# The down projection of a hybrid encoder as seven block products in three groups of channel tiles

## The chip, the cores and the metric

The kernel runs on one core of a Trainium2 chip. The time is device microseconds of one execution. TensorE (PE) multiplies; VectorE (DVE), ScalarE (ACT) and GpSimd (POOL) do elementwise work; SyncE (SP) issues the transfers (DMA). SBUF holds the operands, PSUM the sums of TensorE, in banks of 512 float32 columns by 128 partitions.

## The reference

A sequence of 512 positions with 1024 channels goes through two layers. Each has a mixer (Fourier group and windowed attention, then an output projection) and a feed-forward part, in float32:

```python
h = rmsnorm(x, norm2[l])
up = dwconv_centred(h @ w_up[l], conv_w[l], conv_b[l])   # 1024 -> 2 x 2816, 3 taps along the positions
gate, val = up[..., :D_FF], up[..., D_FF:]
x = x + (jax.nn.silu(gate) * val) @ w_down[l]            # 2816 -> 1024
```

The change is in the last line, and in what is prepared for layer 1 beside it.

## The kernel before

Activations lie transposed: a tile has 128 channels on the partitions and the 512 positions along the row. `x` is eight such tiles (`x0` to `x7`). The hidden width of 2816 is 22 channel tiles (`FT`).

**Products in three terms.** Each float32 operand is split into a high part that TensorE takes in its faster format and a low part, the rest (`split`, L98; `wsplit` for weights, L132). ACT rounds the high part (`whi`, L90), DVE subtracts for the low part (`wlo`, L93). `mm3` (L114) then issues three matmuls into one bank: high by high (L120), low by high (L121), high by low (L122). Every weight tile goes through this: it is loaded into `wraw` (three buffers of 1024 columns), split into pairs of `whi` and `wlo` (five buffers each, of up to 512 columns) and used.

**The feed-forward part** (from L705) runs twice per layer, over 11 channel tiles each (`HALVES`). An *up phase* goes over the channel tiles. For each it computes two output tiles, gate and value, here called two z: 24 matmuls of 512 columns; an evacuation that multiplies by the norm's factor (DVE, `tF<-ps,rb`); a scaling with bias on ACT; two conv steps on DVE (L96, 511 columns, the second depends on the first). Then Silu on ACT, the gate product (on DVE in layer 0, on POOL in layer 1), and a split of the result into `gu`. A *down phase* then goes over the eight output tiles m: 33 products (11 channel tiles in three terms) of 512 columns into one bank, and one addition of the bank into `x[m]`. In the last phase of the kernel each finished tile is written out, the last one in two halves of 256 columns. PSUM banks go round over six (`FFN_BANKS`).

**Presplit.** While layer 0's feed-forward part runs, `presplit` (L149) prepares layer 1's mixer weights: a load into an `m4` buffer for two pieces, for some a fold (two or three sums), a split into `tA` buffers (six), and two stores to `kept` in DRAM. The generator is advanced at places in the program (every third z, and twice for each m), which set its priority. Layer 1 then loads the split pieces.

**What sets the order.** The program is written in the order above, but a scheduler reorders each engine's instructions when the program is built, by priority and free buffers. On the chip each engine takes its own list strictly in order, and waits at an instruction until its inputs and its buffer are there.

## Time and profile before

| | |
|---|---|
| median of 3 runs | 1057.82 us (1056.07 to 1059.76) |
| the profiled execution | 1056.14 us |
| its span | 1054.3 us |
| matmuls recorded | 5107 |
| bytes moved | 140.03 MB |

The span is the time from the first to the last recorded event of the profiled execution; the execution's own time has 1.8 us around it. In the profile's rows a line "L93" is the line of the helper that issued the instruction, so groups are told apart by their tiles: `wlo<-wraw,whi` is the low part of a weight, `tF<-ps,rb` the evacuation of an up tile, `x<-x,ps` the addition of a down tile. A group's row gives, after its name, busy us and mean ns of one, then the idle time of the engine before them and what ended it. A row of the timeline gives start, duration, engine and instruction; durations of neighbours overlap on TensorE and on DVE, so the rate is read from the starts.

### The profile page before, as it was taken

Reading aid. Unit: us, or ns where it says so; the run is one execution under the profiler, and the core shown is the slowest. Engines: PE = TensorE matmul, PEld = TensorE weight load, DVE = VectorE, ACT = ScalarE, POOL = GpSimd, SP = SyncE. Lnnn points to the kernel's source line nnn. Section 1 sums busy time; section 2 is a strip of 40 time slices with the busy share of each in tenths; the row PEclk is TensorE's granted clock in tenths of the full one; section 3 lists DMA queues with packets and bytes.
Section 4 is the critical chain, followed back from the end, with each engine's and each line's share of the span. In section 5 each row is a group of like instructions: output and inputs, shape, how many; then the busy total and the mean of one; then the engine's idle time right before and its main releaser. Section 6 shows DMA issues by size and latency. Waiting matters only on the chain.

```text
span 1054.3 us, 14425 instructions
## 1 busy us (share of the span) xinstructions
PE 1038.2 (98%) x5107; PEld 873.2 (83%) x5107; DVE 726.8 (69%) x1384; ACT 507.9 (48%) x939; POOL 90.8 (9%) x164
## 2 busy tenths in 40 slices
PE   8998999999999999999999999999999999999998
PEld 8986778888888888888899887888888888888887
DVE  8878768697767777777519775478877336878632
ACT  5339755455444445455423785246554224454421
POOL 0004410000000000000000152001101000101100
PEclk9999999999999999999999999999999999999999
DMA  7232152332269833239856313333332333332241
GB/s 273 83 115 87 58 193 81 100 100 96 78 226 353 324 100 101 89 114 322 280 181 221 113 62 99 122 100 94 101 101 74 96 115 100 98 101 82 82 150 48
DMA packets 60475, 140.03 MB, mean 133 GB/s; under 512 B 6642, under 2 KB 22258, under 8 KB 60404
## 3 DMA queue, kind: packets, MB, share of 16 engines
q1 hardware_dynamic: 60404, 139.12, 40.5%
q8 instruction: 40, 0.66, 0.3%
q14 instruction: 31, 0.25, 0.1%
HBM read 116.02 MB, written 23.07 MB: 132 GB/s over the span
## 4 chain that ended last, share of the span: by engine, by line
PE 93%; DVE 2%; DMA 2%; ACT 1%; issue 1%; POOL 0%; SPq 0%; ACTq 0%; DVEq 0%; POOLq 0%
PE ps L122 28%; PE ps L120 28%; PE ps L121 28%; PE ps L118 3%; PE ps L548 2%; PE ps L541 2%; PE ps L529 1%; DMA wraw<-in_w_qkv_dram 1%; PE ps L234 1%; PE ps L227 1%; ACT tA L90 0%; DMA x<-in_xT_dram 0%; DVE tA L533 0%; ACT act L90 0%; PE ps L500 0%
## 5 line engine op out<-in xcount | busy, mean ns | idle before, releaser
L90 ACT ACTIVATE whi<-wraw 128x512 fp32r<-128x512 f32 (+1 forms) x296 | 182.0, 616 | 290.8 <-PE ps L122 278.4
L120 PE MATMUL ps<-act,whi 128*128 128x512 f32 x768 | 298.9, 390 | 0.0
L121 PE MATMUL ps<-act,wlo 128*128 128x512 f32 x768 | 298.3, 389 | 0.0
L122 PE MATMUL ps<-act,whi 128*128 128x512 f32 x768 | 298.2, 389 | 0.0
L93 DVE TENSOR_TENSOR wlo<-wraw,whi 128x512 fp32r<-128x512 f32 (+1 forms) x304 | 219.7, 726 | 103.4 <-ACT whi L90 102.0
L122 PEld LDWEIGHTS ps<-act,whi 128*128 128x128 f32 x768 | 144.2, 188 | 30.1
L120 PEld LDWEIGHTS ps<-act,whi 128*128 128x128 f32 x768 | 144.2, 188 | 29.7
L121 PEld LDWEIGHTS ps<-act,wlo 128*128 128x128 f32 x768 | 144.2, 188 | 29.7
L96 DVE SCALAR_TENSOR_TENSOR tF<-tF,pb,tF 128x511 f32<-128x511 f32 x176 | 133.5, 763 | 11.1 <-ACT tF L90 8.7
L93 DVE TENSOR_TENSOR tF<-ps,rb 128x512 f32<-128x512 f32 x104 | 71.2, 689 | 77.9 <-PE ps L122 64.7
L120 PE MATMUL ps<-slab,whi 128*128 128x512 f32 (+2 forms) x212 | 82.2, 388 | 0.0
L122 PE MATMUL ps<-slab,whi 128*128 128x512 f32 (+2 forms) x212 | 79.9, 380 | 0.4 <-DVE slab L93 0.3
L121 PE MATMUL ps<-slab,wlo 128*128 128x512 f32 (+2 forms) x212 | 80.0, 378 | 0.0
L90 ACT ACTIVATE tF<-tF,pb 128x512 f32<-128x512 f32 x88 | 71.7, 816 | 11.3 <-DVE tF L93 4.6
L93 DVE TENSOR_TENSOR x<-x,ps 128x512 f32<-128x512 f32 (+1 forms) x49 | 32.9, 674 | 36.5 <-PE ps L122 36.3
L93 POOL TENSOR_TENSOR tF<-tF,tF 128x512 f32<-128x512 f32 x22 | 30.2, 1371 | 256.1 <-DVE tF L96 224.1
L120 PE MATMUL ps<-pT,whi 128*128 128x512 f32 (+1 forms) x132 | 50.5, 383 | 0.0
L121 PE MATMUL ps<-pT,wlo 128*128 128x512 f32 (+1 forms) x132 | 50.5, 383 | 0.0
L122 PE MATMUL ps<-pT,whi 128*128 128x512 f32 (+1 forms) x132 | 50.5, 383 | 0.0
L538 POOL TENSOR_SCALAR tA<-tA,den 128x256 f32<-128x256 f32 (+1 forms) x64 | 37.4, 590 | 145.1 <-DVE den L537 144.6
L533 DVE CUSTOM_DVE_ANT_0 tA<-ps,pb,nsink 128x256 f32<-128x256 f32 (+1 forms) x64 | 37.8, 603 | 14.5 <-PE ps L529 9.7
L122 PEld LDWEIGHTS ps<-slab,whi 128*128 128x128 f32 x212 | 39.7, 188 | 8.3 <-DVE slab L93 0.9
(178 smaller groups left out, 1485.0 us busy)
## 6 DMA issues: line engine op xcount, KB each, us to landing
wraw<-in_w_up_dram SPq DMA_DIRECT2D x88, 512.0 KB, 3.5
wraw<-in_w_down_dram SPq DMA_DIRECT2D x32, 512.0 KB, 3.7
kept<-tA SPq DMA_DIRECT2D x56, 256.0 KB, 5.7
whi<-kept SPq DMA_DIRECT2D x28, 256.0 KB, 3.0
wlo<-kept SPq DMA_DIRECT2D x28, 256.0 KB, 3.0
kept<-tA SPq DMA_DIRECT2D x32, 192.0 KB, 4.4
wraw<-in_w_down_dram SPq DMA_DIRECT2D x32, 192.0 KB, 2.4
wraw<-in_w_o_dram SPq DMA_DIRECT2D x8, 512.0 KB, 3.7
```

The lines of the kernel that those rows point to most:

```text
L90: return nc.scalar.activation(out, in_, func, **kw)
L93: return (eng or nc.vector).tensor_tensor(out, a, b, op=op)
L96: return nc.vector.scalar_tensor_tensor(out=out, in0=a, scalar=s, in1=b, op0=op0, op1=op1)
L118: nc.tensor.matmul(out, a[0], b[0], start=start, stop=stop, **kw)
L120: nc.tensor.matmul(out, a[0], b[0], start=start, stop=False, **kw)
L121: nc.tensor.matmul(out, a[1], b[0], start=False, stop=False, **kw)
L122: nc.tensor.matmul(out, a[0], b[1], start=False, stop=stop, **kw)
L227: nc.tensor.matmul(pt[:, 2 * b:2 * b + 2], acc[:, b * P:(b + 1) * P], ones2, start=True, stop=True)
L533: nc.vector.tensor_tensor_reduce(out=pr[:, :n], in0=sc[:, :n], in1=mask[:, m0:m0 + n], scale=qs_scale[p][:, i, e:e + 1], scalar=nsink[:, l ...
L538: nc.gpsimd.tensor_scalar(pr[:, :n], pr[:, :n], den[:, i:i + 1], 1.0, op0=ALU.mult, op1=ALU.mult)
L541: tr = nc.tensor.transpose(pp[:, j * P:(j + 1) * P], pr[:, j * P:(j + 1) * P], ident)
L548: pv = nc.tensor.matmul(py[64 * e:64 * e + 64, i0 * P:(i1 + 1) * P], vp[:, j, 64 * g:64 * g + 64], pT[:, half, e, b0:b0 + 2 * (i1 - i0) + ...
```

## The change

The down projection takes two output tiles and two halves of the channel tiles and of the positions as a 2 x 2 block product, in Strassen's scheme (Winograd's form): seven block products in the place of eight, and 15 sums. With weights A, activations B, the sums are

- weights, per output pair: S1 = A21 + A22, S2 = A11 - S1, S3 = A11 - A21, S4 = A12 + S2, over up to 512 columns, on DVE (`tF<-wraw`);
- activations, per channel pair: T1 to T4 over 256 columns, on DVE (`seven_gu`), once per group;
- results: the products stand in three half banks X, Y, Z that go on accumulating, and after each product its half bank is added into a 256-column half of an `x` tile: seven additions per output pair.

A product is 3 matmuls of 256 columns for each channel pair. All seven weight operands are split like any weight. The groups are 8, 8 and 6 channel tiles (`GROUPS`), so a layer has three up and three down phases. A channel tile's partner is half a group further, so up tiles are computed in the order 0, 4, 1, 5 and so on. The gate product is on DVE in both layers. In the last group of layer 1 the output goes out in halves of 256 columns as soon as they have landed. Presplit takes its pieces one by one through a tag of its own, `praw` (two buffers of 512 columns), and is advanced at every z and once for each down phase.

```diff
-HALVES = [(0, 11), (11, 11)]
+GROUPS = [(0, 8), (8, 8), (16, 6)]
...
-             "tA": (512, 6), "tF": (512, 6), "sq": (512, 2)}
+             "tA": (512, 6), "tF": (512, 6), "sq": (512, 2), "praw": (512, 2)}
...
+        def load(src):
+            raw = temp(512, "praw")[:, :src.shape[-1]]
+            nc.sync.dma_start(raw, src)
+            return raw
...
+        for n, (key, _) in enumerate(jobs):
+            raw = got
+            if n + 1 < len(jobs):
+                got = jobs[n + 1][1]()
+            keep(key, fold_wu(raw) if key[0] == "u" else fold_wf(raw) if key[0] == "f" else raw)
+            yield
...
+    def pieces(kp):
+        for tag, n in (("slab", 2), ("pT", 5), ("m4", 2)):
+            for _ in range(TEMPS[tag][1]):
+                whole = temp(512 * n, tag, F32R)
+                yield from [whole[:, i * 512:(i + 1) * 512] for i in range(n)]
+
+    def seven_gu(b1, b2, room):
+        t13, t24 = temp(512, "tF"), temp(512, "tF")
+        lo, hi = slice(0, 256), slice(256, 512)
+        tt(t13[:, lo], b1[:, hi], b1[:, lo], ALU.subtract)
+        tt(t13[:, hi], b2[:, hi], b1[:, hi], ALU.subtract)
+        tt(t24[:, lo], t13[:, lo], b2[:, hi], ALU.subtract)
+        tt(t24[:, hi], t24[:, lo], b2[:, lo], ALU.add)
+        g = {}
+        one = next(room)
+        g["B11"] = [one[:, lo], one[:, hi]]
+        split(*g["B11"], b1[:, lo])
+        for src, keys in ((b2, ("B21", "B22")), (t13, ("T1", "T3")), (t24, ("T2", "T4"))):
+            two = [next(room), next(room)]
+            split(*two, src)
+            for key, cols in zip(keys, (lo, hi)):
+                g[key] = [z[:, cols] for z in two]
+        return g
+
+    def seven_w(l, m, f0, kp):
+        n = kp * P
+        a, b = [wload(t["w_down"][l, m + i, :, f0 * P:f0 * P + 2 * n], 2 * n) for i in range(2)]
+        a11, a12, a21, a22 = a[:, :n], a[:, n:], b[:, :n], b[:, n:]
+        yield "X", wsplit(a11), "B11", 0, 0
+        s1 = temp(n, "tF")
+        tt(s1, a21, a22, ALU.add)
+        yield "Y", wsplit(s1), "T1", 1, 1
+        s2 = temp(n, "tF")
+        tt(s2, a11, s1, ALU.subtract)
+        yield "X", wsplit(s2), "T2", 0, 1
+        yield "Z", wsplit(a12), "B21", 0, 0
+        s3 = temp(n, "tF")
+        tt(s3, a11, a21, ALU.subtract)
+        yield "X", wsplit(s3), "T3", 1, 1
+        s4 = temp(n, "tF")
+        tt(s4, a12, s2, ALU.add)
+        yield "Y", wsplit(s4), "B22", 0, 1
+        yield "X", wsplit(a22), "T4", 1, 0
...
-                    if (2 * n + z) % 3 == 2:
-                        next(ahead)
+                    next(ahead)
...
-                tt(ys_[0], ys_[0], ys_[1], ALU.mult, nc.gpsimd if l else nc.vector)
+                tt(ys_[0], ys_[0], ys_[1], ALU.mult)
...
+            for mp in range(KT // 2):
+                if mp == 0:
+                    next(ahead)
+                xy, zz = [psum(FFN_BANKS[(nps[0] + i) % len(FFN_BANKS)]) for i in (1, 2)]
+                nps[0] += 2
+                bank = dict(X=xy[:, :256], Y=xy[:, 256:], Z=zz[:, :256])
+                for i, (b, w, g, r, c) in enumerate(seven_w(l, 2 * mp, f0, kp)):
+                    m, q0 = 2 * mp + r, 256 * c
+                    for k in range(kp):
+                        mm3(bank[b], [z[:, k * P:(k + 1) * P] for z in w], gu[k][g], k == 0 and i in (0, 3), k == kp - 1,
+                            skip_group_check=True)
+                    tt(x[m][:, q0:q0 + 256], x[m][:, q0:q0 + 256], bank[b], ALU.add)
```

Where the first down phase of layer 0 begins, TensorE had this before: the end of the last up tile (`ps_644`), then the first output tile (`ps_665`) on channel tile after channel tile (`slab`, `pT`, `m4`). These are the first and the last rows of that tile's piece and the start of the next tile:

```order
L122 MATMUL ps_644_2905<-act_412_1873,whi_642_2901 128x512
L120 MATMUL ps_665_2975<-slab_447_2008,whi_658_2961 128x512
L121 MATMUL ps_665_2975<-slab_447_2008,wlo_659_2962 128x512
...
L120 MATMUL ps_665_2975<-m4_626_2843,whi_663_2971 128x512
L121 MATMUL ps_665_2975<-m4_626_2843,wlo_664_2972 128x512
L122 MATMUL ps_665_2975<-m4_626_2843,whi_663_2971 128x512
L120 MATMUL ps_683_3044<-slab_447_2008,whi_676_3030 128x512
```

Thirty matmuls on ten channel tiles, and as many of the next tile, stand ahead of those on the eleventh (`m4_647`).

At the start of layer 0's second down phase TensorE now has the last up tile (`ps_978`), the product A11 B11 into X (in `ps_996`, weights `whi_1000`, `wlo_1001`), and then S1 T1 into Y, in the other half of that bank (weights `whi_1003`, `wlo_1004`):

```order
L122 MATMUL ps_978_4252<-act_412_1873,whi_976_4248 128x512
L120 MATMUL ps_996_4322<-slab_811_3599,whi_1000_4328 128x256
...
L122 MATMUL ps_996_4322<-m4_933_4084,whi_1000_4328 128x256
L120 MATMUL ps_996_4322<-slab_812_3602,whi_1003_4347 128x256
L121 MATMUL ps_996_4322<-slab_812_3602,wlo_1004_4348 128x256
```

Twelve matmuls stand between the last up tile and the first that takes the high part of S1, and one more ahead of the first that takes its low part. The other five group starts have the same form, with nine matmuls in the groups of six.

DVE had this at the first of these two places before: the evacuation of the last up tile (`tF_645`), its conv steps, gate product and low part, with low parts of down weights and presplit's pieces (`tA`) between them:

```order
L93 TENSOR_TENSOR wlo_677_3031<-wraw_675_3028,whi_676_3030 128x512
L93 TENSOR_TENSOR tF_645_2930<-ps_644_2905,rb_418_1893 128x512
L93 TENSOR_TENSOR wlo_679_3035<-wraw_675_3028,whi_678_3034 128x512
L96 SCALAR_TENSOR_TENSOR tF_646_2932<-tF_645_2930,pb_96,tF_646_2932 128x511 x2
L93 TENSOR_TENSOR wlo_682_3041<-wraw_680_3038,whi_681_3040 128x384
L93 TENSOR_TENSOR tF_634_2883<-tF_634_2883,tF_646_2932 128x512
L93 TENSOR_TENSOR m4_647_2938<-tF_634_2883,m4_647_2938 128x512
L93 TENSOR_TENSOR wlo_695_3100<-wraw_693_3097,whi_694_3099 128x512
L93 TENSOR_TENSOR tA_654_2952<-m4_652_2949,tA_653_2951 128x384
```

The low parts of the first two output tiles' weights stand around the evacuation, not behind what follows from it.

At the second place DVE now has the evacuation of the last up tile (`tF_979`), a sum of the activations, the addition of the first product into `x0`, the conv steps, the gate product, and two sums:

```order
L93 TENSOR_TENSOR tF_979_4277<-ps_978_4252,rb_418_1893 128x512
L93 TENSOR_TENSOR tF_986_4295<-tF_941_4124 128x256
L93 TENSOR_TENSOR x0_74<-x0_74,ps_996_4322 128x256
L96 SCALAR_TENSOR_TENSOR tF_980_4279<-tF_979_4277,pb_96,tF_980_4279 128x511 x2
L93 TENSOR_TENSOR tF_967_4228<-tF_967_4228,tF_980_4279 128x512
L93 TENSOR_TENSOR tF_986_4295<-tF_967_4228,tF_941_4124 128x256
L93 TENSOR_TENSOR tF_987_4296<-tF_986_4295,tF_967_4228 128x256
```

Right behind these come S1 (`tF_1002`), low parts of the activations (`m4_988`, `m4_989`), another sum, S2 (`tF_1005`), S3 (`tF_1010`), the low part of S1 (`wlo_1004`), and later the low part of A12 (`wlo_1009`):

```order
L93 TENSOR_TENSOR tF_1002_4345<-wraw_999_4326 128x512
L93 TENSOR_TENSOR m4_988_4303<-tF_967_4228,m4_988_4303 128x512
L93 TENSOR_TENSOR tF_987_4296<-tF_987_4296,tF_967_4228 128x256
L93 TENSOR_TENSOR m4_989_4306<-tF_986_4295,m4_989_4306 128x512
L93 TENSOR_TENSOR tF_1005_4364<-wraw_998_4324,tF_1002_4345 128x512
L93 TENSOR_TENSOR tF_1010_4400<-wraw_998_4324,wraw_999_4326 128x512
L93 TENSOR_TENSOR wlo_1004_4348<-tF_1002_4345,whi_1003_4347 128x512
L93 TENSOR_TENSOR m4_990_4309<-tF_987_4296,m4_990_4309 128x512
L93 TENSOR_TENSOR tF_1013_4419<-wraw_998_4324,tF_1005_4364 128x512
L93 TENSOR_TENSOR wlo_1007_4367<-tF_1005_4364,whi_1006_4366 128x512
L93 TENSOR_TENSOR wlo_1009_4384<-wraw_998_4324,whi_1008_4383 128x512
```

S1 and its low part moved behind everything that follows from the last up tile. Presplit's last piece (`tA_1220<-praw_1206`) now stands ahead of the evacuation of the last up tile of layer 0's first group; before, its pieces stood in both down phases of layer 0.

More of the change, by code (lines that the diff above doesn't have):

```diff
@@ L163, in store @@
                 late.pop()()
-        def cols(src, n, step):
-            def load():
-                raw = temp(1024, "m4")
-                nc.sync.dma_start(raw[:, :n], src)
-                return [raw[:, c:c + step] for c in range(0, n, step)]
-            return load
-        def prepare(kind, raw):
-            if kind == "u":
-                return fold_wu(raw)
-            return fold_wf(raw) if kind == "f" else raw
+        def load(src):
+            raw = temp(512, "praw")[:, :src.shape[-1]]
+            nc.sync.dma_start(raw, src)
+            return raw
@@ L189, in presplit @@
-        got = jobs[0][0]()
-        for n, (_, keys) in enumerate(jobs):
-            for i, key in enumerate(keys):
-                keep(key, prepare(key[0], got[i]))
-                if i == len(keys) - 1 and n + 1 < len(jobs):
-                    got = jobs[n + 1][0]()
-                yield
+            for m in range(KT):
+                jobs.append((f"o{half}{m}", lambda h=half, m=m: load(t["w_o"][l, h, :, m * 512:(m + 1) * 512])))
+        got = jobs[0][1]()
+        for n, (key, _) in enumerate(jobs):
[4 more added lines that the diff above has]
+            yield
```

61 lines of the change are left out of this document (20 added, 41 removed).

## The prediction

> **What bounds the kernel now.** I read the page first: busy shares, then the chain of work that ended last.
>
> ```profile
> PE 1038.2 (98%) x5107; PEld 873.2 (83%) x5107; DVE 726.8 (69%) x1384; ACT 507.9 (48%) x939; POOL 90.8 (9%) x164
> PE 93%; DVE 2%; DMA 2%; ACT 1%; issue 1%; POOL 0%; SPq 0%; ACTq 0%; DVEq 0%; POOLq 0%
> ```
>
> TensorE is the chain; VectorE, at 69%, is the only engine that could take over. The waits of TensorE (longest first, total, times, longest) say how little else is late:
>
> ```profile
> PE ps L274 <- ACT sq L90: 2.7, 1, 2.7
> ...
> PE ps L122 <- DVE slab L93: 0.3, 1, 0.3
> ```
>
> The second row is all that TensorE ever waits where an up phase hands over to a down phase: matmuls on other channels cover the wait for the last channel. Next, the timeline of TensorE at the end, where the last output tile is taken in halves of 256 columns, as the change takes all of them:
>
> ```profile
> 1030.07 0.39 PE L120 MATMUL ps<-slab,whi 128*128 128x512 f32 x1
> ...
> 1042.76 0.39 PE L122 MATMUL ps<-m,whi 128*128 128x512 f32 x1
> 1042.98 0.28 PE L120 MATMUL ps<-slab,whi 128*128 128x256 f32 x1
> ...
> 1050.78 0.28 PE L122 MATMUL ps<-m,whi 128*128 128x256 f32 x1
> ```
>
> Durations overlap, so starts count: 56 steps of 512 columns in 12.69 us are 226.6 ns each, 65 steps of 256 in 7.80 us are 120.0 ns. Half the columns cost 53%.
>
> **The matmuls.** Down projection of a layer before: 22 x 8 x 3 = 528 matmuls of 512 columns, 119.6 us. After: 4 output pairs x 11 channel pairs x 7 products x 3 = 924 of 256 columns, 110.9 us. Over two layers TensorE loses 17.5 us of work. The Trainium skill ("TensorE: Matmul & The Clock Gate", Back-to-back issue gap) gives N/2.4 + 2.5 ns, 215.8 and 109.2 ns; the rows lie 11 ns above both, and by the rule the saving would be 26 us.
>
> **VectorE, in bulk.** Prices come from a crowded stretch and from rows with the shapes that are added:
>
> ```profile
> 218.00 1.41 DVE L96 SCALAR_TENSOR_TENSOR tF<-tF,pb,tF 128x511 f32<-128x511 f32 x2
> 219.32 0.69 DVE L93 TENSOR_TENSOR tF<-ps,rb 128x512 f32<-128x512 f32 x1
> 219.92 0.68 DVE L93 TENSOR_TENSOR wlo<-wraw,whi 128x512 fp32r<-128x512 f32 x1
> 220.52 0.69 DVE L93 TENSOR_TENSOR tF<-tF,tF 128x512 f32<-128x512 f32 x1
> ...
> 342.39 0.76 DVE L93 TENSOR_TENSOR tA<-m 128x256 f32<-128x256 f32 x2
> ...
> 487.10 0.55 DVE L93 TENSOR_TENSOR wlo<-wraw,whi 128x384 fp32r<-128x384 f32 x1
> 487.56 0.68 DVE L93 TENSOR_TENSOR tA<-m,tA 128x512 fp32r<-128x512 f32 x1
> L93 DVE TENSOR_TENSOR x<-x,ps 128x256 f32<-128x256 f32 x2 | 0.8, 422 | 6.8 <-PE ps L122 6.8
> ...
> L90 ACT ACTIVATE whi<-wraw 128x512 fp32r<-128x512 f32 x256 | 161.2, 631 | 252.6 <-PE ps L122 247.7 <-DMA wraw<-in_w_down_dram 2.0 <-PE ps L118 1.3
> ```
>
> Back to back an instruction of 512 columns takes 0.60 us, a conv step 0.66, 384 columns 0.46, 256 columns 0.34 (two of 0.42 in 0.76). One output pair of a group of eight needs 4 sums, 7 low parts and 7 additions into x: 11 x 0.60 + 7 x 0.34 = 9.0 us beside 84 x 0.120 = 10.1 us of matmuls. In the group of six it is 7.4 beside 7.6. In an up phase, four z (two channels) need 17 x 0.60 + 8 x 0.66 + 5 x 0.34 = 17.2 us (the gate product, on POOL in layer 1 before, is in it) beside 96 x 0.2266 = 21.8. So in bulk the added work is covered, though barely. The order in which it stands is what it costs.
>
> **Start of a down phase.** The changed order puts one product (A11 x B11, 12 matmuls, 1.4 us) behind the up phase on TensorE, then S1 x T1. On VectorE the low part of S1 stands at the end of a chain that starts with the evacuation of the last up tile. Before, 60 matmuls that don't need the last channel stood there, 13.6 us. The steps, from an undisturbed z and its neighbours:
>
> ```profile
> 365.69 0.69 DVE L93 TENSOR_TENSOR tF<-ps,rb 128x512 f32<-128x512 f32 x1 [1.30 <-PE ps L122]
> 366.35 0.69 DVE L93 TENSOR_TENSOR wlo<-wraw,whi 128x512 fp32r<-128x512 f32 x1
> 367.26 1.54 DVE L96 SCALAR_TENSOR_TENSOR tF<-tF,pb,tF 128x511 f32<-128x511 f32 x2 [0.22 <-ACT tF L90]
> ...
> 1043.18 0.69 DVE L93 TENSOR_TENSOR x<-x,ps 128x512 f32<-128x512 f32 x1 [3.65 <-PE ps L122]
> ```
>
> Let 0 be the start of the first product. The last row starts 0.42 us after the last matmul of 512 columns did (1042.76), so the evacuation starts at 0.2. The conv pair starts 1.57 after it (ACT's scaling lies between), but an addition into x stands before it that waits for the first product (its last matmul starts at 1.32 and takes 0.28): pair from 1.97 to 3.5. Gate product, dependent: 4.2. Two dependent sums of 0.42: 5.1. Then, at the crowded rate, S1's sum, a low part, a sum of 256, a low part, S2, S3: 3.3 us. The low part of S1 itself runs from 8.4 to 9.1. TensorE, done at 1.4 and with one matmul (0.1) on the high part in between, waits 7.5 us. Nothing fills that: the rows behind on TensorE need the same or later low parts. With 384 columns the same count gives 7.2. In layer 0's first group the conv pairs of two earlier z and a low part stand in the chain too, and B11 of the last pair comes late: 1.8 more by the same steps. Six starts: 4 x 7.5 + 1.8 + 2 x 7.2 = 46.2 us.
>
> **The refill behind it.** VectorE owes four more instructions of 0.60 before the third product's low part: TensorE is done with S1 x T1 at 10.6, the low part at 11.5: 1 us. The first product of the next output pair needs 9 instructions more, some 4.9 us, while TensorE has 2.9 us of products: 2 us. Its second weight tile has no free buffer (three, two held by the current pair) until A12's low part is made, and lands this much later:
>
> ```profile
> wraw<-in_w_down_dram SPq DMA_DIRECT2D x32, 512.0 KB, 3.7
> wraw<-in_w_down_dram SPq DMA_DIRECT2D x32, 192.0 KB, 2.4
> ```
>
> 11.5 + 3.7 = 15.2, where VectorE (three low parts and an addition on, 2.1 us) would have come to it at 13.6: up to 1.6 more. Bounds 0 and 4.6 us; I take 3.5 for a group of eight and 2.6 for one of six, since VectorE has a tenth to spare from there on: 4 x 3.5 + 2 x 2.6 = 19.2 us.
>
> **Presplit.** The 44 weight pieces of layer 1 now all stand on VectorE before the end of layer 0's first up phase (32 low parts without folding, 16 of them 384 wide, and 12 folds with theirs: about 33.5 us). Two stretches of before (from and to, length, then busy us of PE, PEld, DVE, ACT, POOL) and the stores:
>
> ```profile
> 150.00:176.00 26.00, 26.00 (x124) 21.75 (x123) 17.61 (x30) 11.86 (x20) 1.02 (x1) 1.00 0.23 79
> 176.00:204.00 28.00, 28.00 (x133) 23.44 (x132) 17.52 (x29) 12.59 (x21) 1.01 (x1) 1.00 0.36 113
> ...
> kept<-tA SPq DMA_DIRECT2D x56, 256.0 KB, 5.7
> ```
>
> From 150 to the end of eight channels (87 us from 204) are 141 us; the load is 35 + 4 x 17.2 + 33.5 = 137, in order, each piece behind a load and behind a buffer whose store takes 5.7 us. TensorE then waits for 0 (all fits) to 15 us (33.5 + 68.8 - 87, nothing fits early). I take 8, the middle, since neither row decides.
>
> Costed at nothing: the extra output transfers (same last size as now), the norm work beside layer 0's last group (the next projection's matmuls stand between its products), ACT (7 high parts of 0.63 in 10 us).
>
> **Sum.** -17.5 + 46.2 + 19.2 + 8 = +55.9. The profiled execution took 1056.1 (span 1054.3), 1.7 under the median 1057.8: **1112 us**. A measurement of this kernel tells 0.3% (3 us) from no change.
>
> **Rivals.** *Starts alone*: the refill and the presplit fit in after all, as the bulk sums allow: 1056.1 - 17.5 + 46.2 = 1085. Chance 0.17. *The clock drops in each wait*: the rows show a slow start,
>
> ```profile
> 8.09 0.52 PE L121 MATMUL ps<-whi,act 128*128 128x384 f32 x1
> 8.41 0.48 PE L120 MATMUL ps<-whi,act 128*128 128x384 f32 x1
> 8.73 0.34 PE L121 MATMUL ps<-whi,act 128*128 128x384 f32 x1
> 8.90 0.33 PE L120 MATMUL ps<-whi,act 128*128 128x384 f32 x1
> ```
>
> with 0.32 us a step until 8.73 and 0.17 after it. If 7 us of idleness bring that back and six us of work end it (the first matmul starts at 2.69), half of six us is lost six times: 18 us, less what falls into the refill's waits anyway: up to 1130. For it: no wait in this trace is over 2.7 us, so it isn't excluded. Against it: one matmul stands in each wait. Chance 0.18. The Trainium skill ("TensorE: Matmul & The Clock Gate", Why this matters for your kernels) speaks of idle gaps over about 3 us that return the clock to half; no wait here is long enough to show it. *Other side, faster*: the chain is shorter than I count because VectorE, with 10% to spare, reaches S1's low part within the first product, as before where 0.3 us was waited; then only the matmuls count, 1056 - 17.5 = 1039, and with presplit's 8 still 1047. It decides below 17.5/6 = 2.9 us a start. Against it: the chain holds the evacuation, scaling, conv pair and gate product of one tile, 4 us by rows, before any sum. Chance 0.05. *VectorE saturates in the down phases* is priced in the refill; the 9.0 beside 10.1 us speak against more.
>
> **Numbers.** Likeliest, 0.60, 1095 to 1125. Range 1080 to 1134: it takes in starts alone (1085, less 5 if one wait in the chain hides) and the clock (1130, and 4 for presplit above its middle); left out are the faster rival and sums that miss both ways, under 0.2. Faster 0.05, same 0.02, slower 0.93.
>
> **What would show it.** Right: TensorE's waits list rows of the down matmul on DVE's wlo, six of about 7 us; 256-column steps of 120 ns; in windows of the down phases TensorE below 85%, VectorE near 90%. Wrong: waits of the six starts under 3 us (the chain), a granted clock under 0.97 (the clock), or TensorE idle in mid up phases of layer 1 (a cause not listed).

## The result and the profile after

The changed kernel took 1156.71 us (median of 4 runs, 1154.2 to 1160.4) against 1056.98 us for the kernel before on the same chip: ratio 1.0943, 95% interval 1.0928 to 1.0958. The forecast was 1112 with a range of 1080 to 1134: the sign was right, the size 45 us too small. The profiled execution took 1156.34 us, its span is 1154.5, 100.2 us longer than before.

The page of after, busy shares, the granted clock in 40 slices, and the chain that ended last:

```profile
PE 1052.4 (91%) x5866; PEld 913.0 (79%) x5866; DVE 903.7 (78%) x1841; ACT 561.6 (49%) x1055; POOL 63.2 (5%) x142
PE   8999998993699996999789999999979999799977
PEclk9999999997799998999899999999989999899989
PE 68%; DVE 16%; DMA 9%; ACT 4%; issue 2%; POOL 0%; SPq 0%; DVEq 0%; ACTq 0%; POOLq 0%
```

TensorE's share of the chain fell from 93% to 68%; VectorE has 16% of it and transfers 9%. The slices in which TensorE is low are the starts of down phases, and the clock is low there too. The longest waits of TensorE (total us, times, longest):

```profile
PE ps L120 <- ACT whi L90: 29.2, 8, 4.8
PE ps L121 <- DVE wlo L93: 27.4, 17, 3.0
PE ps L120 <- ACT m L90: 14.6, 1, 14.6
PE ps L120 <- ACT pT L90: 5.8, 1, 5.8
PE ps L120 <- DVE x L93: 5.5, 9, 1.1
```

The first two rows are mostly the starts of the six down phases and what follows them. The third and fourth are one place, the first down phase of layer 0. A normal start, in the timeline of TensorE at layer 1's first group:

```profile
847.51 0.28 PE L122 MATMUL ps<-m,whi 128*128 128x256 f32 x1
852.59 0.58 PE L120 MATMUL ps<-slab,whi 128*128 128x256 f32 x1 [4.81 <-ACT whi L90]
855.22 0.58 PE L121 MATMUL ps<-slab,wlo 128*128 128x256 f32 x1 [2.04 <-DVE wlo L93]
855.59 0.41 PE L122 MATMUL ps<-slab,whi 128*128 128x256 f32 x1
855.81 0.41 PE L120 MATMUL ps<-pT,whi 128*128 128x256 f32 x1
```

From 847.51 to 855.22, less two steps of 0.12, TensorE loses 7.5 us. Then it runs at 0.21 us a step in place of 0.12. Layer 0's first group, the same view:

```profile
268.99 0.28 PE L122 MATMUL ps<-slab,whi 128*128 128x256 f32 x1
275.11 0.58 PE L120 MATMUL ps<-pT,whi 128*128 128x256 f32 x1 [5.84 <-ACT pT L90]
...
290.85 0.58 PE L120 MATMUL ps<-m,whi 128*128 128x256 f32 x1 [14.59 <-ACT m L90]
```

Here the first product itself waits, for the activations of its third and fourth channel pair. VectorE's timeline says why:

```profile
265.29 0.69 DVE L93 TENSOR_TENSOR tA<-praw,tA 128x512 fp32r<-128x512 f32 x1 [0.83 <-ACT tA L90]
...
272.30 0.69 DVE L93 TENSOR_TENSOR tA<-praw,tA 128x512 fp32r<-128x512 f32 x1 [1.16 <-ACT tA L90]
...
285.13 0.69 DVE L93 TENSOR_TENSOR tA<-praw,tA 128x512 fp32r<-128x512 f32 x1
285.74 2.07 DVE L96 SCALAR_TENSOR_TENSOR tF<-tF,pb,tF 128x511 f32<-128x511 f32 x3
287.72 0.68 DVE L93 TENSOR_TENSOR tF<-ps,rb 128x512 f32<-128x512 f32 x1
```

The last row is the evacuation of the last up tile, which TensorE finished at 268.4: VectorE came to it 19 us late, with pieces of presplit (`tA`) ahead of it on its list.

**How the loss is counted below.** For each down phase I take the time from its first matmul to its last and subtract its matmuls at the undisturbed steps (120.0 ns for 256 columns, 226.6 for 512; some up tiles of the next group stand between). What is left is time that TensorE lost there, waits and slow steps together. Before, it is 0.0 us in each of the four down phases. After, it is 37.3, 15.8 and 17.4 us in layer 0 and 12.9, 13.3 and 15.6 in layer 1: 112.3 us. With 6.2 us lost at the beginning of layer 0's first up phase that is 118.5; less the 17.5 us of matmuls saved it makes 101, against 100.2 measured.

### The profile page after: what moved, and what is told of

It is laid out like the page before. It is cut to its first block, busy times and chain, and to the rows that moved or that the text cites. A ratio compares the mean times of both kernels' runs of the same rounds, so it can differ in the third digit from the quotient of the medians.

```text
span 1154.5 us, 16570 instructions
## 1 busy us (share of the span) xinstructions
PE 1052.4 (91%) x5866; PEld 913.0 (79%) x5866; DVE 903.7 (78%) x1841; ACT 561.6 (49%) x1055; POOL 63.2 (5%) x142
## 4 chain that ended last, share of the span: by engine, by line
PE 68%; DVE 16%; DMA 9%; ACT 4%; issue 2%; POOL 0%; SPq 0%; DVEq 0%; ACTq 0%; POOLq 0%
PE ps L120 20%; PE ps L121 20%; PE ps L122 20%; DVE tF L93 5%; DMA wraw<-in_w_down_dram 4%; DVE wlo L93 4%; PE ps L118 3%; DMA praw<-in_w_o_dram 2%; DVE x L93 2%; DVE tF L96 1%; DMA praw<-in_w_qkv_dram 1%; PE ps L595 1%; ACT tA L90 1%; DVE tA L93 1%; PE ps L588 1%
## 5 line engine op out<-in xcount | busy, mean ns | idle before, releaser
L90 ACT ACTIVATE whi<-wraw 128x512 fp32r<-128x512 f32 (+1 forms) x272 | 166.6, 616 | 220.3 <-PE ps L122 211.2
L93 DVE TENSOR_TENSOR wlo<-wraw,whi 128x512 fp32r<-128x512 f32 (+1 forms) x280 | 186.1, 669 | 37.9 <-ACT whi L90 35.9
L120 PE MATMUL ps<-slab,whi 128*128 128x256 f32 (+2 forms) x272 | 90.2, 336 | 33.5 <-ACT whi L90 27.7
L93 DVE TENSOR_TENSOR x<-x,ps 128x256 f32<-128x256 f32 (+1 forms) x184 | 81.0, 441 | 46.9 <-PE ps L122 42.1
L121 PE MATMUL ps<-slab,wlo 128*128 128x256 f32 (+2 forms) x272 | 88.6, 326 | 27.6 <-DVE wlo L93 27.4
L90 ACT ACTIVATE whi<-tF 128x512 fp32r<-128x512 f32 (+1 forms) x96 | 57.0, 594 | 90.5 <-PE ps L122 69.6
L122 PE MATMUL ps<-slab,whi 128*128 128x256 f32 (+2 forms) x272 | 85.9, 318 | 0.4 <-DVE slab L93 0.3
L120 PE MATMUL ps<-pT,whi 128*128 128x256 f32 x264 | 78.6, 298 | 5.8 <-ACT pT L90 5.8
L121 PEld LDWEIGHTS ps<-slab,wlo 128*128 128x128 f32 x272 | 53.9, 198 | 34.3 <-DVE wlo L93 32.0
L121 PE MATMUL ps<-pT,wlo 128*128 128x256 f32 x264 | 78.3, 297 | 0.0
L93 DVE TENSOR_TENSOR wlo<-tF,whi 128x512 fp32r<-128x512 f32 (+1 forms) x96 | 61.3, 643 | 8.4 <-ACT whi L90 6.8
L122 PE MATMUL ps<-pT,whi 128*128 128x256 f32 x216 | 63.6, 294 | 0.0
```

The lines of the kernel that those rows point to most:

```text
L90: return nc.scalar.activation(out, in_, func, **kw)
L93: return (eng or nc.vector).tensor_tensor(out, a, b, op=op)
L120: nc.tensor.matmul(out, a[0], b[0], start=start, stop=False, **kw)
L121: nc.tensor.matmul(out, a[1], b[0], start=False, stop=False, **kw)
L122: nc.tensor.matmul(out, a[0], b[1], start=False, stop=stop, **kw)
```

## The experiments

Theory: three costs, each by latency or order on VectorE's list (presplit's pieces about 30 us in layer 0, the starts, the refill behind them). Rivals: the clock costs by itself; VectorE simply has too much work, wherever it stands. The loss in the six down phases in us, as counted above, in all kernels that are built from the changed one (a classical down phase has eight block products, as before):

| kernel | median us | layer 0 | layer 1 |
|---|---|---|---|
| changed kernel | 1156.7 | 37.3, 15.8, 17.4 | 12.9, 13.3, 15.6 |
| no splits | 1135.0 | 14.8, 13.8, 17.4 | 16.0, 13.6, 15.6 |
| paced pieces | 1145.5 | 24.9, 18.2, 17.2 | 15.2, 14.2, 15.9 |
| own ring for sums | 1159.8 | 33.1, 9.0, 38.2 | 9.2, 9.1, 12.1 |
| filler matmuls (5.4 us each, counted as lost) | 1157.6 | 35.0, 13.4, 19.9 | 13.8, 12.3, 17.8 |
| early up tile | 1149.0 | 34.1, 10.1, 17.4 | 10.9, 11.0, 19.0 |
| paced, own ring, early tile | 1113.6 | 18.8, 12.7, 19.3 | 5.2, 5.8, 11.5 |
| the same, sums on POOL | 1135.6 | 21.1, 13.8, 23.2 | 12.1, 9.8, 13.1 |
| the same three, groups of six classical | 1086.7 | 18.2, 13.1, 0.0 | 4.3, 5.1, 0.0 |
| that, no splits | 1070.7 | 5.2, 5.7, 0.0 | 4.6, 6.5, 0.0 |
| seven products in layer 1's eights alone | 1060.9 | 0.0, 0.0, 0.0 | 4.2, 5.7, 0.0 |
| that, two early tiles, fourth weight buffer, pieces in the weights' ring | 1105.95 | 4.0, 3.5, 0.0 | 2.5, 3.5, 0.0 |
| the same, pieces in the ring of the norm's squares | 1055.6 | 0.0, 0.0, 0.0 | 2.8, 3.5, 0.0 |

The kernel before had medians of 1056.98 to 1057.6 beside these. Now one by one.

**No splits.**

```diff
-            two = [temp(n, "tA", F32R) for _ in range(2)]
-            split(two[0], two[1], src)
+            two = [nil[:, :n]] * 2        # zeros; nothing is loaded
```

> Leaves out the splits of layer 1's mixer weights (their loads, folds, high and low parts); zeros are stored in their place, so the mixers of layer 1 compute on zeros. Theory A (the 44 pieces stand early on VectorE's list, behind their own loads and stores, and everything behind them is late): the first group of layer 0 loses its 24 us behind the up phase and the 6 us in it, about 30 us of 1156.7, so 1127. Theory B (the stall of that group comes from the new pieces of the gate tiles, which wait for buffers, not from presplit): 1150 or more. Theory C (VectorE has too much work in layer 0, wherever it stands): the 33.5 us of pieces fall out of a saturated engine, also some 30 us here; the paced kernel tells it from A.

Measured: 1135.0, ratio 1.0734 (1.0718 to 1.075). Layer 0's first group lost 14.8 us instead of 37.3, and its first up phase was 6.0 us shorter (112.8 us for 118.8): together 28.5 us, near the 30 that theories A and C both gave. 6.5 us of it went at the start of the kernel, where layer 0's mixer began later in this schedule. Theory B falls; A and C are left.

**Paced pieces.**

```diff
-                    stt(y[:, :-1], u[:, 1:], ...)
+                    conv = stt(y[:, :-1], u[:, 1:], ...)
-                    next(ahead)
+                    with tc.issue_after(conv.ins):
+                        next(ahead)
```

> Each of the 44 pieces is put behind the conv pair of its own up tile on VectorE, so the same work is spread over the whole feed-forward part of layer 0 and none stands early. Theory A (the place on the list, not the amount, costs 30 us): 20 to 30 us less than the changed kernel, 1127 to 1137, and TensorE's waits in layer 0's first group fall to about 10 us, like the other groups. Theory C (amount): the loss only moves to the later up phases, within 6 us of 1156.7. Theory B (gate pieces' buffers): within 6 us too, with the same waits on the high part of the last pair.

Measured: 1145.5, ratio 1.0841 (1.0821 to 1.0861). Only 11 us came back, between the two theories. The windows show what pacing did. Columns: stretch, length, busy us of PE, PEld, DVE, ACT, POOL with counts, granted clock, DMA share, GB/s. Before, in the first up phase:

```profile
204.00:294.00 90.00, 90.00 (x399) 74.53 (x398) 73.57 (x112) 48.55 (x73) 0.00 (x0) 1.00 0.29 92
```

After, the same phase and the start behind it:

```profile
200.00:268.00 68.00, 67.52 (x306) 55.82 (x305) 59.43 (x114) 38.76 (x66) 1.39 (x1) 1.00 0.84 287
268.00:290.00 22.00, 2.42 (x12) 1.77 (x10) 19.90 (x34) 11.41 (x20) 3.44 (x6) 0.64 0.73 251
```

Paced:

```profile
200.00:262.00 62.00, 62.00 (x275) 51.35 (x274) 56.62 (x101) 38.23 (x65) 0.00 (x0) 1.00 0.65 200
262.00:284.00 22.00, 7.55 (x36) 6.60 (x35) 20.99 (x40) 10.54 (x19) 0.00 (x0) 0.64 0.50 149
```

And without splits, again the up phase and the start behind it:

```profile
200.00:268.90 68.90, 68.90 (x309) 57.16 (x308) 58.46 (x99) 37.67 (x60) 0.60 (x1) 1.00 0.28 89
268.90:290.00 21.10, 11.65 (x77) 10.94 (x76) 18.50 (x34) 8.26 (x14) 0.00 (x0) 0.84 0.18 51
```

In the changed kernel all 44 pieces stood ahead of the evacuation that ends the first up phase, and transfers took 84% of the DMA engines' time (29% before). On its list VectorE stood waiting for the half of a piece that ACT makes. From 150 to 295 us:

```profile
DVE tA L93 <- ACT tA L90: 18.3, 16, 3.9
```

With pacing that wait is 0.2 us from 144 to 284 us, transfers take 65%, and the up phase gets its 6 us back. So the place of the pieces cost the 11 us. The other 17 of the 28.5 us go only when the pieces go. It isn't shown how much of them is the amount of work (theory C) and how much the place that the paced pieces have. The busy share of VectorE doesn't decide it: in the up phase it is 85% without splits, 87% in the changed kernel and 91% with pacing.

**Own ring for the weight sums.** S1 becomes S2 and S4 in the same tile of a ring of two (`sq`).

```diff
-        s1 = temp(n, "tF")
+        s1 = temp(n, "sq")
...
-        s2 = temp(n, "tF")
+        s2 = s1
...
-        s4 = temp(n, "tF")
+        s4 = s2
```

> The weight sums S1, S2 and S4 are made in a ring of two tiles of their own, each in place of the one before, instead of the ring that the evacuation and the convolution use. Theory A (S1's low part stood at the end of the chain only because of the shared ring): S1 and its parts are made early, the start of T1 then waits for the last pair's T1 alone, two sums at 5.1 us and a high part of 0.6, so about 4.3 us instead of 7.5: 6 x 3.2 = 19 us less, 1138; if the clock then stays up, another 10 to 18 us less. Theory B (the wait is set by the last pair's own chain, sums aside): under 5 us of change.

Measured: 1159.8, ratio 1.096 (1.093 to 1.0989): no gain in sum. But each group of eight except the first lost 4 to 7 us less (15.8 to 9.0, 12.9 to 9.2, 13.3 to 9.1), and layer 1's group of six 3.5 less, near the 3.2 per start of theory A. Layer 0's group of six gave it all back (17.4 to 38.2): the norm's squares use that ring too, and stand behind the sums there. The first group started 6 us later as well. In the later kernels layer 0's group of six keeps the old ring.

**Filler matmuls.** 24 matmuls into an unread bank behind the first product, recorded as `ps<-act` at L798.

```diff
-                        mm3(bank[b], ...)
+                        last = mm3(bank[b], ...)      # mm3 now returns its last matmul
...
+                    if mp == 0 and i == 0:
+                        idle = psum("tp")
+                        with tc.issue_after(last.ins):
+                            for _ in range(24):
+                                nc.tensor.matmul(idle, h2[0][:, 0, :P], h2[0][:, 0, :], start=True, stop=True)
```

> 24 matmuls into a bank that nobody reads stand behind the first product of each down phase (5.4 us of the 7.5 us wait), on tiles that are long there. Nothing else changes. Theory A (TensorE's clock falls to half because it idles, and the half clock costs some 3 us in each of six starts): the granted clock behind the starts stays at 1.0, 15 to 20 us less than the changed kernel, 1137 to 1142, with the start waits themselves no shorter. Theory B (the slow steps behind a start are TensorE waiting for operands, and the clock costs nothing): 1155 to 1160, with small waits in place of slow steps.

Measured: 1157.6, ratio 1.0953 (1.0931 to 1.0976), the changed kernel's time, with a mean granted clock of 0.979 for 0.966: 50 us at half the clock for 80. So theory A fell for the 30 us that went. At layer 1's second group the changed kernel had these stretches (the clock is the third number from the end):

```profile
986.50:996.00 9.50, 2.65 (x16) 2.15 (x15) 8.79 (x17) 4.88 (x8) 0.00 (x0) 0.74 0.00 0
996.00:1010.00 14.00, 13.90 (x93) 13.42 (x93) 12.09 (x24) 5.08 (x9) 0.00 (x0) 0.81 0.37 108
```

and with the filler:

```profile
986.10:996.10 10.00, 8.15 (x46) 6.92 (x45) 9.30 (x17) 4.91 (x8) 0.00 (x0) 1.00 0.00 0
996.10:1010.00 13.90, 12.66 (x101) 12.14 (x101) 12.37 (x25) 5.57 (x9) 0.00 (x0) 1.00 0.39 114
```

The clock stays at 1.00, TensorE is done sooner with each step and waits instead, and VectorE is as busy as before (12.1 and 12.4 us): the phase took 62.5 us instead of 63.5. Here, where VectorE set the pace, half the clock on TensorE cost 1 us. The 50 us at half the clock that are left, nearly half of them in layer 0's first group, were taken away by no run alone.

**Presplit alone**, in the kernel before.

```diff
-            for kk in range(KT // 2):
-                jobs.append((cols(t["w_qkv"][l, grp, kk], 768, 384), [...]))
+            for k in range(KT):
+                jobs.append((f"qkv{grp}{k}", lambda g=grp, k=k, c=c: load(...)))
...
-                    if (2 * n + z) % 3 == 2:
-                        next(ahead)
+                    next(ahead)
```

> The kernel before, with one part of the change alone: the 44 pieces of layer 1's mixer weights are loaded and split one by one in tiles of their own, early, as in the changed kernel; down projection and halves stay as they were. The runs so far gave presplit 22 us in the changed kernel. Theory A (the pieces alone hold VectorE up behind their loads and stores): 1065 to 1080, with TensorE waiting at the end of layer 0's first half. Theory B (they only hurt together with the sums, because a classical down phase has 60 matmuls of other channels to cover a late last pair): 1056 to 1061.

Measured: 1063.96, ratio 1.0066 (1.0046 to 1.0085). Near theory B, but not free: 6.5 us. The end of the mixer with the beginning of the up phase, and the rest of the up phase, are in this kernel:

```profile
150.00:204.00 54.00, 50.43 (x219) 39.59 (x218) 42.05 (x80) 27.94 (x51) 1.02 (x1) 0.97 0.81 256
204.00:303.00 99.00, 99.00 (x445) 81.96 (x444) 89.70 (x157) 59.30 (x100) 4.78 (x7) 1.00 0.81 279
```

The loss is at the beginning of the up phase, as in the changed kernel; the down phase behind it lost 0.0 us, though VectorE was 91% busy and waited for ACT's halves of pieces here too (17.0 us from 150 to 304). That the 60 matmuls in front cover this is argued from the order; no run took them away alone.

**Groups alone**, in the kernel before.

```diff
-HALVES = [(0, 11), (11, 11)]
+HALVES = [(0, 8), (8, 8), (16, 6)]
```

> The kernel before, with one part of the change alone: groups of 8, 8 and 6 channel tiles instead of two halves of 11, with the classical eight block products. Theory A (a start of a down phase costs about 0.3 us as long as matmuls on other channels stand first, so a third group costs next to nothing): 1056 to 1060. Theory B (each boundary between the phases costs by itself, as weights are loaded and VectorE's list turns over): 7 us for each of two more boundaries, 1068 or more.

Measured: 1058.44, ratio 1.0014 (1.0004 to 1.0023). A third group costs some 1 to 1.5 us in the whole kernel, and no down phase loses anything. What a start costs is due to the seven products and their order.

**Early up tile.** `up_tile` is the body of the loop over z.

```diff
+            if f0 + nf < FT:
+                first = [up_tile(f0 + nf, 0)]
             nxt = []
             for mp in range(KT // 2):
```

> The changed kernel, but the first up tile of the next group is computed in front of the down phase (four of the six starts; the last group of a layer has no next one). Its 24 matmuls of 512 columns are 5.4 us of work on TensorE that don't need the last pair. Theory A (the start wait is latency of the last pair's chain): the tile fills it, 5 us in each of three groups and more in layer 0's first, 15 to 25 us less, 1132 to 1142. Theory B (VectorE's amount of work sets the length of a down phase): the tile's own low parts, evacuation and convolution (5 instructions, 3.1 us) go into the same list, the wait moves behind the first products, under 6 us gained.

Measured: 1149.0, ratio 1.0869 (1.0847 to 1.0892): 8 us, between the theories. The four groups with a tile in front lost 2 to 6 us less. The start did not vanish, since S1's parts stayed at the end of VectorE's list and the tile brought five instructions more into it; layer 1's group of six, with no tile in front, lost 3.4 us more.

**All three.** The diffs of the paced pieces, of the own ring and of the early tile together, the ring with one exception:

```diff
-        s1 = temp(n, "sq")
+        s1 = temp(n, "sq" if l or kp == 4 else "tF")
```

> Three edits at once: paced presplit, weight sums in tiles of their own (but in layer 0's group of six, where that ring serves the norm), and the early up tile. By the runs so far: pacing gave 11 us; the own sums took 4 to 7 us from each group of eight and 3.5 from layer 1's group of six (20 us), which was lost again elsewhere; the early tile should fill what is left of four start waits. Theory A (the costs are separate latencies): 1156.7 - 11 - 20 - 10 = about 1115. Theory B (VectorE's amount sets the pace once the latencies are gone): 1130 or more, with VectorE over 95% busy in the down phases.

Measured: 1113.6, ratio 1.0524 (1.0501 to 1.0548), as theory A had it. In layer 1's groups of eight the own ring alone left 9.2 us and the tile alone 10.9; together they left 5.2 (first group). One brings the operand forward, the other fills what is left. The work on VectorE is the same in all of these, so most of the loss there came from the order.

**Sums on POOL**, on top of all three.

```diff
-        tt(s1, a21, a22, ALU.add)
+        tt(s1, a21, a22, ALU.add, nc.gpsimd)
```

and so for S2, S3 and S4.

> The kernel with all three edits (1113.6), and the four weight sums of an output pair made on POOL instead of VectorE: an instruction of this shape took 1.37 us there in the profile of before, so 5.5 us beside 10.1 us of products, and POOL is idle. VectorE's list for an output pair falls from 9.0 to 6.6 us. Theory A (once the order is mended, the amount of VectorE's work sets what is still lost): the loss in the six down phases, 73 us in the trace, falls by half, 1080 to 1095. Theory B (latency of single operands sets it: S1, S2 and S4 are a chain, three times 1.37 us plus the crossings between the engines): 1110 to 1125, with TensorE waiting for S2's and S4's parts.

Measured: 1135.6, ratio 1.0742 (1.0721 to 1.0763), 22 us slower than with the sums on VectorE. Two things happen, and how the 22 us divide between them was not measured. The sums are 1.34 to 1.42 us each on average, three of them in a chain; and VectorE itself is slowed. Its rows in layer 1's first group without and with POOL's sums (us in total, mean ns):

```profile
L93 DVE TENSOR_TENSOR wlo<-wraw,whi 128x512 fp32r<-128x512 f32 x17 | 11.5, 689 | 3.5 <-ACT whi L90 3.4
L96 DVE SCALAR_TENSOR_TENSOR tF<-tF,pb,tF 128x511 f32<-128x511 f32 x4 | 3.0, 750 | 0.0
```

```profile
L93 DVE TENSOR_TENSOR wlo<-wraw,whi 128x512 fp32r<-128x512 f32 x18 | 14.2, 794 | 3.1 <-ACT whi L90 3.0
L96 DVE SCALAR_TENSOR_TENSOR tF<-tF,pb,tF 128x511 f32<-128x511 f32 x4 | 4.0, 996 | 0.0
```

**Groups of six classical**, the three edits in the groups of eight. The classical branch is that of the kernel before.

```diff
+                seven = nf == 8
...
+                if not seven:
+                    two = [next(room), next(room)]
+                    split(*two, ys_[0])
+                    gu.append(two)
```

> The kernel with all three edits (1113.6), but the group of six of each layer takes the classical eight block products. It loses 2.4 us of saved matmuls in each layer. Theory A (a group pays for its start, not for its products; the two groups of six, which have no next up tile in front, lose 19.3 and 11.5 us in the trace): 1113.6 - 30.8 + 4.8 = 1088. Theory B (layer 0's group of six is slow by the norm and the next projection beside it, not by the scheme): 1098 or more.

Measured: 1086.7, ratio 1.0268 (1.0241 to 1.0295), theory A. A group of eight saves 192 x 226.6 ns less 336 x 120.0 ns, 3.2 us. The table's losses nearly give the kernel: 40.7 us lost less 4 x 3.2 saved is 27.9, on 1057.3, or 1085.2.

**That without splits.** The edit of the first run, on the kernel of the last one.

```diff
-            split(two[0], two[1], src)
+            two = [nil[:, :n]] * 2
```

> The kernel with seven products in all groups of eight (1086.7), with the splits of layer 1's mixer weights left out (zeros are stored in their place, so layer 1's mixers compute on zeros). Theory A (the pieces, even paced, are what makes layer 0's groups dearer than layer 1's): the two groups of layer 0 lose about 5 us each as in layer 1, instead of 18.2 and 13.1 us, and the kernel comes to 1066, or up to 1072 if layer 0's mixers start some 6 us later, as they did in the first run without splits. Theory B (something else in layer 0): 12 us and more in each of these groups still, 1080 or more.

Measured: 1070.7, ratio 1.0123 (1.0107 to 1.0138), theory A at its upper end (the mixer began later again). Layer 0's groups now lose what layer 1's lose. So presplit, even paced, is all that made layer 0 dearer: 13.0 and 7.4 us. By the prices of the prediction it should fit: 17.2 us of work for four z and at least 2.4 for four pieces, beside 21.8 us on TensorE. The busy share of VectorE in the up phase doesn't tell the two kernels apart either: 62.7 of 71 us with the pieces, 65.6 of 73 without. How far it is behind does. TensorE finished the last tile in front of the first product at 271.1 us with the pieces, and VectorE came to its evacuation at 281.6; without them it was 273.0 and 273.4. VectorE is 10.5 us late with no more than 88% of its time in use.

**Seven products in layer 1's groups of eight alone.**

```diff
-                seven = nf == 8
+                seven = l and nf == 8
```

The early tile stands in front of these two down phases only.

> The seven products in layer 1's two groups of eight alone, with own sums and early up tile; everything else takes eight products, with the pieces of presplit paced. By the trace of the kernel with the seven in all groups of eight, these two groups lose 4.3 and 5.1 us and save 3.2 each. Theory A (losses and savings add up, and the two groups of layer 0 cost 18.2 + 13.1 - 6.4 = 25 us there): 1086.7 - 25 = 1062, 2 to 5 us above the kernel before. Theory B (what is lost in layer 0 is presplit's own amount of work and stays without the seven products): 1070 or more.

Measured: 1060.9, ratio 1.0033 (1.0023 to 1.0044), theory A. Layer 0's classical down phases lose 0.0 us with the paced pieces in front of them.

**Two early tiles and a fourth weight buffer.**

```diff
-            raw = temp(512, "praw")[:, :src.shape[-1]]
+            raw = wtile()[:, :src.shape[-1]]      # wraw now has 4 buffers
...
-                first = [up_tile(f0 + nf, 0)]
+                first = [up_tile(f0 + nf, z) for z in range(2)][::-1]
```

> As the kernel with seven products in layer 1's two groups of eight alone, with two early up tiles instead of one (10.9 us of matmuls in front of the first product), and a fourth buffer for raw weights (the pieces of presplit share that ring and give up their own). Theory A (the 2 us left at each start and the 2 us wait for A12's low part later in the group are latencies that this covers): the two groups lose 1 us each, 1057.3 + 1.4 for the groups - 6.4 + 2 = 1054, 0.3% below the kernel before. Theory B (VectorE's amount: two tiles in front bring 10 instructions more into the list before the first product's parts, and the wait moves behind): 1060 to 1066.

Measured: 1105.95, ratio 1.0457 (1.0444 to 1.0471), a miss of both theories, in layer 0. The pieces shared the ring of the raw up weights, and those came late. The longest of ACT's waits from 150 to 290 us, and the longest of SyncE's list (total, times, longest):

```profile
ACT whi L90 <- DMA wraw<-in_w_up_dram: 29.4, 14, 4.3
SPq L159 <- ACT tA L90: 38.8, 14, 14.6
```

The second row is stores of pieces that wait for ACT's half. The longest, 14.6 us, ended at 197.7; a load of up weights stood behind it on SyncE's list, was issued at 199.1, and TensorE was idle for 9.7 us until 203.4. Layer 1's groups lost 2.5 and 3.5 us, less than 4.2 and 5.7.

**The same with the pieces in the ring of the norm's squares.**

```diff
-            raw = wtile()[:, :src.shape[-1]]
+            raw = temp(512, "sq")[:, :src.shape[-1]]
```

> Seven products in layer 1's two groups of eight alone, two early up tiles, a fourth buffer for raw weights, and the pieces of presplit loaded into the ring of the norm's squares instead of the raw-weight ring. Theory A (layer 0 then runs as with the seven in layer 1 alone, and layer 1's groups lose 2.5 and 3.5 us as in the run before): 1060.9 - 3.9 = 1057, no difference to the kernel before that could be measured. Theory B (the fourth buffer or the early tiles cost in layer 0 too): 1062 or more.

Measured: 1055.57, ratio 0.9981 (0.9972 to 0.999). It is the only version that isn't slower than the kernel before: 2 us faster, less than the 3 us that the prediction took as the bound of what a measurement tells, though the interval leaves 1 out. So the pieces' place in the weights' ring was what cost the 50 us. Its page is that of a kernel bound by TensorE again:

```profile
PE 1034.1 (98%) x5380; PEld 881.8 (84%) x5380; DVE 784.7 (74%) x1566; ACT 522.7 (50%) x979; POOL 62.1 (6%) x142
PE 90%; DVE 5%; ACT 2%; DMA 1%; issue 1%; POOL 0%; ACTq 0%; DVEq 0%; POOLq 0%
```

Its two groups save 6.4 us of matmuls and lose 6.3, so the 2 us don't come from the seven products; where they come from isn't shown.

## Why the prediction was right in sign and wrong in size

- **Matmuls, -17.5: right.** The step of 256 columns is 120.0 ns in after too. By the rule of the Trainium skill ("TensorE: Matmul & The Clock Gate", Back-to-back issue gap) the estimate was 26; the rows stand 11 ns above it, at 256 columns as at 512.

```profile
891.11 0.28 PE L120 MATMUL ps<-pT,whi 128*128 128x256 f32 x1
...
892.91 0.28 PE L120 MATMUL ps<-m,whi 128*128 128x256 f32 x1
```

Fifteen steps lie in these 1.80 us.

- **Six starts, 46.2: right, in mechanism and size.** The two waits of a start make 7.5 us in groups of eight and 7.1 in groups of six, each time. With layer 0's first group as it is without splits (7.5) that is 44.1. In layer 1's first group the low part of S1 starts 8.3 us after the first product, where the count gave 8.4. The wait itself is split otherwise than the sign said: 4.8 us for the high part from ACT and 2.0 for the low part, not some 7 on the low part alone. That S1 at the end of the chain sets it was shown by the own ring: there the start waits less, and for the last pair's activations.

- **The refill, 19.2: the larger of the two terms that failed, mis-sized by 26 us.** The loss behind the start, slow steps included, is 5.4 and 5.8 us in layer 1's groups of eight, 7.3 and 8.3 in layer 0's (the first one without splits), 8.5 and 10.3 in the groups of six: 45.6 us. The forecast took 3.5 and 2.6, with 4.6 as its bound, "since VectorE has a tenth to spare from there on". That was the step that failed: VectorE does not catch up within one output pair. In layer 1's first group it is busy for 9.3 of 10, 10.7 of 11.8, 10.1 of 12 and 10.3 of 12 us, and TensorE still waits at 873.7 (1.1 us, for an addition into `x`) and at 885.0 (0.9 us, for a low part), 30 us behind the start:

```profile
868.00:880.00 12.00, 10.93 (x91) 10.73 (x91) 10.14 (x20) 4.75 (x8) 0.00 (x0) 1.00 0.36 98
880.00:892.00 12.00, 11.06 (x92) 10.86 (x92) 10.32 (x20) 4.72 (x8) 0.00 (x0) 1.00 0.34 107
892.00:904.00 12.00, 12.00 (x78) 10.94 (x78) 6.25 (x12) 4.00 (x7) 0.00 (x0) 1.00 0.47 146
```

"9.0 beside 10.1" was taken as a tenth to spare. From 846 to 892 VectorE also waits 2.2 us for ACT's halves of weights and 0.7 for a weight tile, and these waits come out of that tenth. About 3.4 of the 5.4 us lie ahead of 868, where the granted clock is 0.78; but in the second group, where the filler kept the clock at 1.00, only 1.0 of 5.8 went. In the groups of six, 7.4 beside 7.6 is no room at all, and they were given the smaller refill.

- **Presplit, 8 with bounds 0 to 15: the other term that failed, mis-sized by 20.5 us.** It cost 28.5 us (the runs without and with splits). The upper bound put VectorE's busy times in a row, as if pieces only took its time, and the wait of a piece for its ACT half stood at nothing. By that count VectorE could be 15 us late at the end of the up phase; it came 19.3 us late to the last evacuation. Of the 137.7 us up to there (from 150) it was busy for 117.9, and the waits for ACT's halves of pieces, 18.3 us, nearly fill the rest. "I take 8, the middle, since neither row decides" was a choice without a row; 15 was no upper bound. Pacing gave back 11 us; what makes the other 17 is open between amount and place.

- **The clock rival: it came, and cost little where a run took it away.** The granted clock fell to half behind every start, in stretches of 3.4 to 27.3 us, and the kernel's mean to 0.966, under the 0.97 that the prediction named as its sign. The section of the Trainium skill named beside it ("TensorE: Matmul & The Clock Gate", Why this matters for your kernels) speaks of idle gaps of about 3 us and more; for waits of 5 us the trace agrees (0.74 from 986.5 to 996.0). A stretch behind a wait of 1.85 us, shown at the end, lies outside it. The price, 3 us a start, was wrong: with the filler some 30 us of half clock went and the time stayed, because VectorE set the pace in the same stretches.

- **VectorE saturates**, which the forecast saw only in the refill, is half right. VectorE does set the pace behind the starts, as the filler showed. But time as such is not what it lacks: in layer 1's groups of eight the same work in another order lost 5.2 and 5.8 us instead of 12.9 and 13.3. *Starts alone* fell: the refill and presplit cost 74 us beside them.

The sum as measured: -17.5 + 44.1 + 45.6 + 28.5 = +100.7, against 100.2 us of span. Of the 45 us that the forecast was short, the refill is 26 and presplit 20.5; the starts were 2 too dear. The matmuls and the starts were no luck, since each step of theirs is found in the trace.

## What to carry to other kernels

A scheme that trades a matmul for sums moves the bound to the engine that makes the sums: compare the work on that engine with TensorE's in each stage, with what else stands on its list there and with its waits for other engines' halves. Here 9.0 beside 10.1 us was late. Look at what the classical order covers for nothing (60 matmuls in front of a late operand), since the new order may have nothing to put there; a gain of 3.2 us per group was smaller than any loss that one start brought, until operands were made early and two tiles of other work stood in front, and then it was just even. When background work gets buffers of its own, ask what held it back until then: in the kernel before, where the pieces shared other buffers and stood in the down phases, no down phase lost anything.

## What the runs showed of the hardware

- TensorE's granted clock fell to half also without a long idle time. With the filler, the longest wait at layer 1's first start is 1.85 us, in the timeline

```profile
851.72 0.28 PE L120 MATMUL ps<-slab,whi 128*128 128x256 f32 x1
853.85 0.39 PE L121 MATMUL ps<-slab,wlo 128*128 128x256 f32 x1 [1.85 <-DVE wlo L93]
```

 and the window behind it has a granted clock of 0.72:

```profile
854.80:867.00 12.20, 11.68 (x75) 11.39 (x74) 10.48 (x21) 4.31 (x7) 0.00 (x0) 0.72 0.30 87
```

 A wait of the same length in layer 1's second group was followed by no such stretch. What decides it stays open.
- The stretches of half clock that end within the changed kernel's trace are multiples of 3.41 us: 3.41, 6.83, 10.24 and 27.31.
- VectorE's instructions took 15% (low parts of weights, 689 to 794 ns) to 33% (conv steps, 750 to 996 ns) longer in a stretch where POOL made sums of 512 columns in SBUF at the same time. The additions of a PSUM bank into `x` did not (419 ns without, 412 with POOL's sums).
